# Twenty modulation tiles of a hybrid SSD and MoE block summed by matmuls on TensorE in place of multiply-adds on VectorE

## Chip, cores and metric

The kernel runs on one core of a Trainium2 chip. The metric is device time of one execution in microseconds (us), lower is better; the figure for a kernel is the median of its runs.

## What is computed

Two transformer-like blocks run one after the other over 256 tokens of width 1024, in fp32. Each block starts from a modulation vector that its condition `c` gives; the vector is cut into six pieces of 1024.

```python
# first block
mod = silu(c) @ w_ada + b_ada                      # w_ada: 1024 x 6144
sh1, sc1, g1, sh2, sc2, g2 = split(mod, 6)
h   = layer_norm(x) * (1 + sc1) + sh1
mix = hybrid_mixer(h, ...)                         # SSD branch + short convolution branch
x   = layer_norm(ALPHA * x + g1 * mix) * ln1_g + ln1_b
h   = layer_norm(x) * (1 + sc2) + sh2
x   = layer_norm(ALPHA * x + g2 * moe_ffn(h)) * ln2_g + ln2_b
# second block: mod = silu(c_2) @ w_ada_2 + b_ada_2, six pieces again; attention, convolved feed-forward
```

The mixer projects `h` with `w_in`: the SSD's conv inputs (4096 columns, a causal convolution of four taps and a silu), a short convolution branch (three groups of 1024 columns, then `w_sc_out`), a gate `z` and two merge gates. The change is about the sums `silu(c) @ w_ada`, for twelve pieces in all.

## The kernel before

All weights come through one stream (`Stream`, L35): tiles of 1 MB (128 x 2048 fp32), loaded by DMAs of the SP queue in the order in which they were requested, into five buffers `wraw`. A buffer is given back when its tile is used up, and the next load waits for that. A tile of a projection carries 256 output columns. It is split in two halves, each into a rounded part `whi` on ScalarE (L196) and a rest `wlo` on VectorE (L200), three buffers of each; `lin_fm` (L548) then runs 24 matmuls per half of 128x128 weights against 256 tokens, three for each of eight k (whi by xh, whi by xl, wlo by xh; L556 to L558). A half is split one half ahead of its use.

The stages that matter, with their places in the span:

- start, up to 36 us: the first two modulation pieces (sh1, sc1), with one tile of weights for two rows-of-128 of `w_ada`. `ada_piece` (L395) sums them on TensorE: per tile eight fp32 matmuls of 32 output rows each, four beside each other in four strips of 32 columns of the array, with the activation broadcast to 32 columns in `cst` (L186) as weights;
- conv inputs, 36 to 144 us: sixteen pairs `xbc_pair` (L621), each one `lin_fm` and then, deferred, the taps on VectorE (L633, six per pair);
- convolution, 144 to 239 us: twelve `lin_fm` (pc, ph, pb; L729), and between them steps of the SSD, a generator (`ssd`, L654) that `step` moves on: masks R on GpSimd, `seg`/`ea` matmuls, exponentials E and Cs on ScalarE, products on VectorE (L691, L706), the `yp` matmuls (L713, L717) that read both;
- branch output, 239 to 283 us: four `lin_fm` (pyb, L765) and the rest of the SSD, whose tail runs on to 288 us beside the first `z` matmuls;
- z, the merge gates, the SSD output projection (pya, L868; to 440 us), and the output matmuls pmix (L912) with `w_o`, which VectorE first multiplies by g1 (L242).

The other ten pieces, forty tiles, are put into the stream between these tiles by the strings `XS, SS, OS, ZS, GS, US` (L270): a 1 at place i puts one tile behind the i-th projection tile of that stage. `ada_tick` (L410) uses it up behind that place's `lin_fm`: a multiply by a per-row scalar into the accumulator `adac` for the first of a piece's eight rows-of-128 (ScalarE, L430), a multiply-add for the others (VectorE, L432), 1024 columns wide for the first seven pieces and in two halves of 512 for the last three. Behind the fourth tile four matmuls with a matrix of ones sum the accumulator over the partitions (L437), VectorE adds the bias (L392) and a DMA of ScalarE's queue writes the row out (L461).

Only SP's order is written out by hand in these stages; the order on the other engines is the framework's schedule from the program's order. TensorE and VectorE then work their queues in order.

Of the kernel before, what the change touches and what calls it, by code (L numbers as in the profile page):

```python
# [18 lines left out]
F32 = mybir.dt.float32  # L19
# [102 lines left out]
def build(ctx, tc, I, out, dbg=None, stop=None):  # L122
# [8 lines left out]
    glob = keep  # L131
# [51 lines left out]
    PE.transpose(pt[:, :16], crow, ident[:16, :16])  # L183
    csil = glob.tile([128, 16], F32, name="csil")
    A.activation(csil, pt[:, :16], AF.Silu)
    cst = glob.tile([128, 8, 32], F32, name="cst")  # L186
    V.tensor_copy(cst, csil[:, :8, None].to_broadcast([128, 8, 32]))


    def splitter(q, hi, lo, v):  # L190
# [70 lines left out]
    def req_ada(b, piece):  # L261
        for k0 in range(0, 8, 2):
# [5 lines left out]
    req_ada(0, 1)  # L268

    XS, SS, OS, ZS, GS, US = [[int(c) for c in a] for a in  # L270
                              "0110110110110110,010101010101,1111,11111111,11111111,10101010".split(",")]
    ada_at = {("x", i): XS[i] for i in range(16)}
    ada_at.update({("s", i): SS[i] for i in range(12)})
    ada_at.update({("o", i): OS[i] for i in range(4)})
# [3 lines left out]
    assert sum(ada_at.values()) == 40  # L278
    ada_tiles = [(b, pc, k0) for b, pc in [(0, n) for n in range(2, 6)] + [(1, n) for n in range(6)] for k0 in range(0, 8, 2)]
    ada_next = [0, 0]  # L280
    ADA_WIDE = 7
    ada_acc = [None, None]

# [106 lines left out]
    def ada_end(b, pc, p):  # L390
        r = work.tile([128, 256], F32, tag="adar", name=f"adar{b}_{pc}", bufs=2)
        V.tensor_add(r, p[:, :256], bada[pc % 2])  # L392
        return r

    def ada_piece(b, pc):  # L395

        ada_bias(b, pc)
        p = paux(f"ada{b}_{pc}")
        for k0 in range(0, 8, 2):
            i = ada_q[b, pc, k0]  # L400
            w = ws.take_raw(i)
            wv = w.rearrange("p (k n) -> p k n", k=2)
            for k in range(2):
                for j in range(4):
                    PE.matmul(p[32 * j:32 * j + 32, :256], cst[:, 8 * b + k0 + k, :], wv[:, k, 256 * j:256 * j + 256],
                              start=(k0 + k == 0), stop=(k0 + k == 7), tile_position=(0, 32 * j))
            ws.done(i)
        return ada_end(b, pc, p)

    def ada_tick(*at):  # L410

        for _ in range(ada_at.get(at, 0)):
            b, pc, k0 = ada_tiles[ada_next[1]]
            n = ada_next[1] // 4
            ada_next[1] += 1
            if k0 == 0:
                ada_bias(b, pc)
                if n < ADA_WIDE:
                    ada_acc[:] = [adac[:, n % 2, 512 * h:512 * h + 512] for h in range(2)]
                else:  # L420
                    ada_acc[:] = [work.tile([128, 512], F32, tag="E", name=f"adae{n}_{h}", bufs=3) for h in range(2)]
            i = ada_q[b, pc, k0]
            wv = ws.take_raw(i).rearrange("p (k n) -> p k n", k=2)
            wide = [(adac[:, n % 2, :], slice(0, D))] if n < ADA_WIDE else \
                [(ada_acc[h], slice(512 * h, 512 * h + 512)) for h in range(2)]
            for k in range(2):
                c = csil[:, 8 * b + k0 + k:8 * b + k0 + k + 1]
                for acc, s_ in wide:
                    if k0 + k == 0:
                        A.activation(acc, wv[:, k, s_], AF.Copy, scale=c)  # L430
                    else:
                        V.scalar_tensor_tensor(acc, wv[:, k, s_], c, acc, op0=OP.mult, op1=OP.add)  # L432
            ws.done(i)
            if k0 == 6:
                p = paux(f"ada{b}_{pc}")
                for j in range(4):
                    PE.matmul(p[32 * j:32 * j + 32, :256], ones_r.bitcast(F32)[:, :32],  # L437
                              ada_acc[j // 2][:, 256 * (j % 2):256 * (j % 2) + 256],
                              start=True, stop=True, tile_position=(0, 32 * j))
                ada_row(ada_end(b, pc, p), b, pc)  # L440
# [1553 lines left out]
```

## Time and profile before

| | |
|---|---|
| median of 3 runs | 1335.69 us (1335.33 to 1337.22) |
| the profiled execution | 1335.36 us |
| its span | 1333.5 us |
| TensorE matmul busy | 1265.9 us, 95% |
| VectorE busy | 813.2 us, 61% |
| ScalarE busy | 562.3 us, 42% |
| mean granted TensorE clock | 0.981 |

The span is that from the first to the last instruction. Busy time of TensorE's matmuls overlaps, since they are pipelined and their ends are modelled, so a busy share near 100% does not say by itself that nothing more fits; the step from one matmul's start to the next does. Each fp32 matmul stands in the trace as two records. L432 is line 432 of the kernel, `adac<-wraw,csil,adac` names what is written and what is read, and "idle before <- releaser" is the time for which an engine sat idle, with what ended that.

### The profile page before, as it was taken

The page shows a single profiled execution, that of the slowest core. Times are in us where ns is not written, and L with a number is a line of the kernel's source. Part 1 is how long each engine was busy: PE and PEld are TensorE (multiplying, and loading weights), DVE is VectorE, ACT ScalarE, POOL GpSimd, SP SyncE. Part 2 cuts the span into 40 slices and gives each one's busy share as a digit, 9 for nine tenths or more (in the row PEclk, how much of TensorE's full clock was granted, in tenths as well). Part 3 has the DMA queues.
Part 4 walks back from the last instruction along what each step waited for, and adds up shares of the span by engine and source line. Part 5 has one row for each costly group of instructions (what it writes and reads, how often), then busy time and mean ns, then how long its engine had stood idle before and what let it go on. Part 6 is the DMA issues. An engine that isn't in the chain of part 4 may idle for free.

```text
span 1333.5 us, 22547 instructions
## 1 busy us (share of the span) xinstructions
PE 1265.9 (95%) x8998; PEld 1026.6 (77%) x8998; DVE 813.2 (61%) x1306; ACT 562.3 (42%) x849; POOL 178.3 (13%) x169
## 2 busy tenths in 40 slices
PE   4999999999999989999999999999979998999997
PEld 2989988789899777657576767476548876999985
DVE  2999998977898852222322222222255677788995
ACT  1666644455654341313131313132245655666643
POOL 1001243421100000211112111112120000000000
PEclk9899999999999969999999999999989999999999
DMA  9977867669789287999999999999995334455450
GB/s 338 323 232 254 263 220 239 226 196 320 250 281 362 78 352 296 406 417 419 419 418 413 400 418 419 378 421 403 418 347 179 126 127 141 144 190 190 161 187 32
DMA packets 148975, 380.18 MB, mean 285 GB/s; under 512 B 7839, under 2 KB 97285, under 8 KB 129028
## 3 DMA queue, kind: packets, MB, share of 16 engines
q1 hardware_dynamic: 145856, 373.20, 75.7%
q0 software_dynamic: 2240, 5.34, 1.2%
q8 instruction: 71, 1.16, 0.4%
q10 hardware_dynamic: 772, 0.19, 0.1%
q14 instruction: 36, 0.29, 0.1%
HBM read 377.59 MB, written 1.10 MB: 284 GB/s over the span
## 4 chain that ended last, share of the span: by engine, by line
PE 61%; DVE 5%; DMA 3%; issue 2%; ACT 1%; POOL 0%; POOLq 0%; DVEq 0%; SPq 0%; ACTq 0%
PE gu L1444 16%; PE dn L1475 8%; PE xgp L1402 5%; PE sc L1497 4%; PE pgt L556 2%; PE pgt L557 2%; PE pgt L558 2%; PE pvl L557 2%; PE pvl L556 2%; PE pvl L558 2%; PE pf L908 1%; PE pf L910 1%; PE pf L906 1%; DVE wlo L200 1%; DMA wraw<-in_w_down_dram 1%
## 5 line engine op out<-in xcount | busy, mean ns | idle before, releaser
L196 ACT ACTIVATE whi<-wraw 128x1024 fp32r<-128x1024 f32 x216 | 228.2, 1059 | 239.6 <-PE pf L910 30.8
L200 DVE TENSOR_TENSOR wlo<-wraw,whi 128x1024 fp32r<-128x1024 f32 x216 | 271.4, 1259 | 64.4 <-ACT whi L196 63.0
L1444 PE MATMUL gu<-mraw,xg 128*32 128x256 f32 (+2 forms) x976 | 135.1, 381 | 0.0
L1485 POOL TENSOR_TENSOR y<-yf,y 128x512 fp32r<-128x512 f32 x60 | 76.9, 1282 | 420.8 <-ACT y L1484 420.7
L1454 DVE SCALAR_TENSOR_TENSOR act<-act,gc,gu 128x256 f32<-128x256 f32 x31 | 14.9, 480 | 192.9 <-ACT act L1453 192.9
L1484 ACT ACTIVATE y<-yf 128x512 fp32r<-128x512 f32 x62 | 39.1, 630 | 160.4 <-DVE yf L1483 160.4
L1444 PEld LDWEIGHTS gu<-mraw,xg 128*32 128x32 f32 (+2 forms) x976 | 86.7, 135 | 22.7 <-issue 5.3
L1444 PE MATMUL gu<-wraw,xg 128*32 128x256 f32 (+2 forms) x704 | 98.7, 381 | 0.0
L1483 DVE TENSOR_TENSOR yf<-dn,g 128x512 f32<-128x512 f32 x62 | 42.9, 692 | 66.2 <-PE dn L1475 66.2
L558 PE MATMUL pl<-hh,wlo 128*128 128x256 f32 x256 | 74.3, 291 | 4.2 <-DVE wlo L200 4.1
L1444 PEld LDWEIGHTS gu<-wraw,xg 128*32 128x32 f32 (+2 forms) x704 | 58.2, 129 | 24.1 <-issue 3.9
L556 PE MATMUL pl<-hh,whi 128*128 128x256 f32 x256 | 73.7, 288 | 0.0
L557 PE MATMUL pl<-hl,whi 128*128 128x256 f32 x256 | 73.5, 288 | 0.0
L432 DVE SCALAR_TENSOR_TENSOR adac<-wraw,csil,adac 128x1024 f32<-128x1024 f32 x49 | 66.4, 1355 | 5.1 <-DMA wraw<-in_w_ada_dram 4.5
L1497 PE MATMUL sc<-y,S 128*128 128x512 f32 x248 | 63.3, 404 | 1.4 <-ACT y L1484 0.8
L1497 PEld LDWEIGHTS sc<-y,S 128*128 128x128 f32 x248 | 45.5, 188 | 17.7 <-issue 4.4
L1453 ACT ACTIVATE act<-gu 128x256 f32<-128x256 f32 x31 | 11.9, 384 | 107.3 <-PE gu L1444 107.3
L1404 ACT ACTIVATE xg<-xgp,mvp 128x512 f32<-128x512 f32 (+1 forms) x64 | 48.8, 765 | 19.4 <-PE xgp L1402 19.2
L1402 PE MATMUL xgp<-D,x2h 128*128 128x512 f32 (+1 forms) x128 | 55.5, 434 | 1.4 <-DVE D L1121 1.4
L1475 PE MATMUL dn<-mraw,aT 128*32 128x512 f32 (+2 forms) x200 | 55.4, 596 | 0.0
L558 PEld LDWEIGHTS pl<-hh,wlo 128*128 128x128 f32 x256 | 49.5, 194 | 6.2 <-DVE wlo L200 5.8
L1402 PE MATMUL xgp<-D,x2l 128*128 128x512 f32 (+1 forms) x128 | 53.8, 421 | 0.1
(575 smaller groups left out, 3522.8 us busy)
## 6 DMA issues: line engine op xcount, KB each, us to landing
wraw<-in_w_in_dram SPq DMA_DIRECT2D x56, 1024.0 KB, 6.2
wraw<-in_w_ada_dram SPq DMA_DIRECT2D x47, 1024.0 KB, 7.6
wraw<-in_w_up_dram SPq DMA_DIRECT2D x44, 1024.0 KB, 5.3
wraw<-in_w_down_dram SPq DMA_DIRECT2D x37, 1024.0 KB, 10.0
mraw<-in_w_up_dram SPq DMA_DIRECT2D x32, 1024.0 KB, 14.5
mraw<-in_w_gate_dram SPq DMA_DIRECT2D x28, 1024.0 KB, 7.1
mraw<-in_w_down_dram SPq DMA_DIRECT2D x23, 1024.0 KB, 17.4
wraw<-in_w_gate_dram SPq DMA_DIRECT2D x21, 1024.0 KB, 15.1
```

What stands on the lines that cost most here:

```text
L196: A.activation(hi, v, AF.Copy)
L200: V.tensor_sub(lo, v, hi.bitcast(F32))
L432: V.scalar_tensor_tensor(acc, wv[:, k, s_], c, acc, op0=OP.mult, op1=OP.add)
L556: PE.matmul(o, wh[:, k, :], xh[:, k0 + k, :], start=(k == 0), stop=False)
L557: PE.matmul(o, wh[:, k, :], xl[:, k0 + k, :], start=False, stop=False)
L558: PE.matmul(o, wl[:, k, :], xh[:, k0 + k, :], start=False, stop=(k == 7))
L1402: PE.matmul(p[:, :c1 - c0], src[:, t, j::8], Dt[:, t, c0:c1], start=(q == 0), stop=(q == 3))
L1404: A.activation(xg[:, j, c0:c1], p[:, :c1 - c0], AF.Identity, scale=mvp[:, 1, j:j + 1], bias=mvp[:, 0, j:j + 1])
L1444: PE.matmul(p[c * k:c * k + c, off:off + 256], xg[:, j, 128 * bb + c * k:128 * bb + c * k + c], wt[j], start=(j == 0), stop=(j == 7), tile ...
L1475: last_dn[0] = PE.matmul(pd[h][c * k:c * k + c, :], aT[:, j, c * k:c * k + c], wt[j][:, 512 * h:512 * h + 512], start=(j == 0), stop=(j == ...
L1485: last_sub[0] = (V if b >= LAST else G).tensor_sub(y[:, 1, hs_], yf[:, h, :], y[:, 0, hs_].bitcast(F32))
L1497: PE.matmul(p, St[:, bb + m, 128 * t:128 * t + 128], y[:, k, 512 * h:512 * h + 512], start=(q == 0), stop=(q == 2 * len(ys) - 1))
```

## The change

Of the forty tiles, the twenty of the first five pieces (g1, sh2, sc2, g2 of the first block, the first piece of the second) are summed as at the start: eight matmuls per tile, 160 in all, into one accumulator in PSUM that stays open over the piece's four tiles. It uses the PSUM bank of the tag "acc". The multiply-adds and the reduction matmuls of these five pieces go. The weights of these matmuls are now the activation's column itself, read 32 times by a broadcast; the tile `cst` and the copy that fills it go, for the first two pieces too. The places shift: twelve tiles beside the conv inputs (ten before), four beside the convolution (six before), four beside the branch output as before, so that the twenty of the first five pieces lie in these three stages. The twenty others stay on VectorE; the last four of them move one place back, behind the second half of each SSD output projection instead of behind the first.

```diff
--- before.py
+++ after.py
@@ -183,8 +183,6 @@
     PE.transpose(pt[:, :16], crow, ident[:16, :16])
     csil = glob.tile([128, 16], F32, name="csil")
     A.activation(csil, pt[:, :16], AF.Silu)
-    cst = glob.tile([128, 8, 32], F32, name="cst")
-    V.tensor_copy(cst, csil[:, :8, None].to_broadcast([128, 8, 32]))
 
 
     def splitter(q, hi, lo, v):
@@ -268,7 +266,7 @@
     req_ada(0, 1)
 
     XS, SS, OS, ZS, GS, US = [[int(c) for c in a] for a in
-                              "0110110110110110,010101010101,1111,11111111,11111111,10101010".split(",")]
+                              "0111101111011110,011011000000,1111,11111111,11111111,01010101".split(",")]
     ada_at = {("x", i): XS[i] for i in range(16)}
     ada_at.update({("s", i): SS[i] for i in range(12)})
     ada_at.update({("o", i): OS[i] for i in range(4)})
@@ -278,6 +276,7 @@
     assert sum(ada_at.values()) == 40
     ada_tiles = [(b, pc, k0) for b, pc in [(0, n) for n in range(2, 6)] + [(1, n) for n in range(6)] for k0 in range(0, 8, 2)]
     ada_next = [0, 0]
+    ADA_PE = 5
     ADA_WIDE = 7
     ada_acc = [None, None]
 
@@ -392,19 +391,23 @@
         V.tensor_add(r, p[:, :256], bada[pc % 2])
         return r
 
+    def ada_rows(p, b, pc, k0):
+
+        i = ada_q[b, pc, k0]
+        wv = ws.take_raw(i).rearrange("p (k n) -> p k n", k=2)
+        for k in range(2):
+            c = csil[:, 8 * b + k0 + k:8 * b + k0 + k + 1].to_broadcast([128, 32])
+            for j in range(4):
+                PE.matmul(p[32 * j:32 * j + 32, :256], c, wv[:, k, 256 * j:256 * j + 256],
+                          start=(k0 + k == 0), stop=(k0 + k == 7), tile_position=(0, 32 * j))
+        ws.done(i)
+
     def ada_piece(b, pc):
 
         ada_bias(b, pc)
         p = paux(f"ada{b}_{pc}")
         for k0 in range(0, 8, 2):
-            i = ada_q[b, pc, k0]
-            w = ws.take_raw(i)
-            wv = w.rearrange("p (k n) -> p k n", k=2)
-            for k in range(2):
-                for j in range(4):
-                    PE.matmul(p[32 * j:32 * j + 32, :256], cst[:, 8 * b + k0 + k, :], wv[:, k, 256 * j:256 * j + 256],
-                              start=(k0 + k == 0), stop=(k0 + k == 7), tile_position=(0, 32 * j))
-            ws.done(i)
+            ada_rows(p, b, pc, k0)
         return ada_end(b, pc, p)
 
     def ada_tick(*at):
@@ -415,6 +418,14 @@
             ada_next[1] += 1
             if k0 == 0:
                 ada_bias(b, pc)
+            if n < ADA_PE:
+                if k0 == 0:
+                    ada_acc[0] = pacc(f"ada{b}_{pc}")
+                ada_rows(ada_acc[0], b, pc, k0)
+                if k0 == 6:
+                    ada_row(ada_end(b, pc, ada_acc[0]), b, pc)
+                continue
+            if k0 == 0:
                 if n < ADA_WIDE:
                     ada_acc[:] = [adac[:, n % 2, 512 * h:512 * h + 512] for h in range(2)]
                 else:
```

## Rows read from the trace of the kernel before

**Rows 1.** The page: busy time by engine; VectorE's busy tenths in 40 equal slices

```profile
PE 1265.9 (95%) x8998; PEld 1026.6 (77%) x8998; DVE 813.2 (61%) x1306; ACT 562.3 (42%) x849; POOL 178.3 (13%) x169
...
DVE  2999998977898852222322222222255677788995
```

**Rows 2.** Busy by stretch: conv inputs; convolution; branch output with the SSD's tail

```profile
core 0: us, PE busy (x) PEld busy (x) DVE busy (x) ACT busy (x) POOL busy (x), PEclk, DMA share, GB/s
35.70:143.70 108.00, 103.78 (x824) 100.53 (x823) 101.23 (x170) 70.46 (x97) 10.96 (x8) 0.96 0.82 271
143.70:239.10 95.40, 90.40 (x760) 85.04 (x760) 90.71 (x108) 47.34 (x68) 33.92 (x22) 1.00 0.72 231
239.10:288.20 49.10, 44.08 (x362) 37.65 (x361) 43.39 (x47) 19.82 (x33) 18.79 (x16) 1.00 0.65 215
```

**Rows 3.** Busy by stretch, same columns: matmuls without a stall; half clock

```profile
57.50:69.00 11.50, 11.50 (x97) 11.40 (x95) 11.50 (x18) 6.83 (x11) 0.00 (x0) 1.00 0.98 319
...
101.70:105.10 3.40, 3.14 (x14) 3.14 (x15) 3.40 (x5) 1.19 (x2) 3.09 (x2) 0.50 0.96 344
```

**Rows 4.** Groups by line, 35.7 to 288.2 us, VectorE: busy, mean ns | idle before

```profile
L200 DVE TENSOR_TENSOR wlo<-wraw,whi 128x1024 fp32r<-128x1024 f32 x67 | 89.5, 1340 | 7.0 <-ACT whi L196 6.9
L432 DVE SCALAR_TENSOR_TENSOR adac<-wraw,csil,adac 128x1024 f32<-128x1024 f32 x41 | 56.1, 1368 | 2.1 <-DMA wraw<-in_w_ada_dram 1.9
```

**Rows 5.** TensorE timeline: start, us; last modulation piece at start, one reduction later

```profile
22.31 1.07 PE L405 MATMUL ada<-wraw,cst 128*32 128x256 f32 x16
...
24.30 1.93 PE L405 MATMUL ada<-wraw,cst 128*32 128x256 f32 x32
...
76.92 0.28 PE L556 MATMUL pl<-hh,whi 128*128 128x256 f32 x1
77.13 0.64 PE L437 MATMUL ada<-adac,ones_r 128*32 128x256 f32 x8
77.70 0.38 PE L557 MATMUL pl<-hl,whi 128*128 128x256 f32 x1
```

**Rows 6.** Who waited for whom, 35 to 143 us: us, times, longest

```profile
PEld pl L558 <- DVE wlo L200: 5.8, 7, 3.1
```

**Rows 7.** The same, 143 to 239 us

```profile
PEld yp L717 <- issue: 4.3, 2, 2.3
PE yp L717 <- DVE Cs L706: 3.9, 2, 2.1
...
PEld ada L437 <- DVE adac L432: 0.5, 1, 0.5
```

**Rows 8.** The same, 239 to 289 us

```profile
PE yp L717 <- DVE Cs L706: 2.3, 2, 1.4
PEld yp L713 <- DVE E L691: 2.3, 3, 1.6
...
PEld btp L698 <- issue: 0.9, 1, 0.9
```

**Rows 9.** VectorE timeline, convolution: start, us, what it ran

```profile
220.00 2.07 DVE L432 SCALAR_TENSOR_TENSOR adac<-wraw,csil,adac 128x1024 f32<-128x1024 f32 x1
221.99 2.06 DVE L200 TENSOR_TENSOR wlo<-wraw,whi 128x1024 fp32r<-128x1024 f32 x1
223.97 0.68 DVE L706 TENSOR_TENSOR Cs<-Cs,BC 128x512 f32<-128x512 f32 x1
```

**Rows 10.** VectorE timeline, output matmuls: start, us [idle before <- releaser]

```profile
413.33 1.42 DVE L432 SCALAR_TENSOR_TENSOR adae<-wraw,csil,adae 128x512 f32<-128x512 f32 x2 [3.33 <-DMA wraw<-in_w_ada_dram]
...
436.86 0.42 DVE L392 TENSOR_TENSOR adar<-ada,bada 128x256 f32<-128x256 f32 x1
...
457.16 0.69 DVE L1028 SCALAR_TENSOR_TENSOR xb<-xb,pmix 128x512 f32<-128x512 f32 x1 [2.72 <-PE pmix L910]
```

**Rows 11.** Who waited for whom, 0 to 36 us

```profile
PEld ada L405 <- DMA wraw<-in_w_ada_dram: 4.3, 4, 1.9
...
PEld ada L405 <- DVE cst L187: 0.9, 1, 0.9
```

## The prediction

> **What bounds the kernel now.** I read the page first. TensorE is busy for 95% of the span, and VectorE's busy tenths stand at 7 to 9 over the first thirteen slices, some 430 us, and mostly at 2 in the MoE [rows 1]. The change lies in that first stretch, so I cut it by stage [rows 2]: conv inputs 108.0 us with VectorE busy for 101.2, convolution 95.4 us with 90.7, branch output and SSD tail 49.1 us with 43.4. VectorE is nearly full in all three. TensorE's busy time is nearly full as well, but it contains the drain of pipelined matmuls, so the step between matmuls decides: 97 matmuls in 11.50 us without a stall [rows 3], 0.119 us each, 5.7 us for the 48 of a weight tile. Sixteen tiles make 91 of the conv inputs' 108 us. So there TensorE is nearly full too, and its holes are what VectorE's lateness leaves. Both engines bound this stretch, one just behind the other: work moved from VectorE to TensorE closes the holes that it pays for and adds its own time.
>
> **The change part by part.** *Off VectorE.* A piece has eight rows-of-128, one on ScalarE and seven on VectorE, so five pieces free 35 multiply-adds. At a mean 1368 ns [rows 4] that is 47.9 us off a queue that is busy for 235.3 of 252.5 us (the sums of rows 2). VectorE drops to about 74% and no longer bounds these stages. This time is not the gain: only TensorE's holes are.
>
> *Onto TensorE.* A reduction, eight records, delays the matmul stream from 76.92 to 77.70, 0.78 us, where an ordinary step takes 0.12: it costs 0.66 us [rows 3, 5]. Thirty-two records of the same shape took 1.93 us and sixteen 1.07 [rows 5], so sixteen more cost 0.86 and eight 0.43. A tile of eight matmuls, sixteen records, thus costs 0.66 + 0.43 = 1.09 us; twenty cost 21.8 us. The bounds are 0.86 (no cost at the borders) and 1.32 (two visits of eight records). The five reductions that go save 5 x 0.66 = 3.3 us. Net +18.5 us, on the path, since the tiles stand in TensorE's own queue.
>
> The border shows in the rows: the first record of the reduction starts 0.21 us after the matmul before it and the next matmul 0.57 us after that [rows 5], where 0.12 and 0.43 would be the plain steps. The Trainium skill, TensorEngine Tiling (Array Packing), section Key Properties, says that changing the tiling mode, not just the tile, drains TensorE; that speaks against this change, which makes forty such switches. The trace agrees, with 0.23 us for a pair of them, and the price of a tile from the rows has them in it already; a drain of the full 0.28 us of a matmul at each border would make it 0.86 + 0.56 = 1.42 us and the sum 6.6 us worse.
>
> *Holes beside the conv inputs.* TensorE waited 5.8 us, in seven places, for `wlo` [rows 6], and one wait was followed by 3.40 us at half clock [rows 3], which costs half of that, 1.7 us. Sixteen splits and taps without the multiply-adds fit easily under the matmuls, so I take both back: -7.5 us (bounds -5.8 and -7.5).
>
> *Holes beside the SSD.* In the convolution the `yp` matmuls waited for Cs: 4.3 us on the weight loads and 3.9 on the matmuls, the same places seen twice, so 4.3; and 0.5 for a reduction's input [rows 7]. In the branch output 2.3 for Cs and 2.3 for E [rows 8]. Together 9.4 us. How much is the multiply-adds' doing? One place read in full: a multiply-add from 220.00 (2.07 us), a split behind it (2.06) and only then Cs at 223.97 [rows 9]. Without the first, Cs comes 2 us earlier and the 2 us stall there is gone. E and Cs also have an exponential and a mask before them which stay. I take 90%, -8.5 us (bounds half of it, -4.7, and all, -9.4).
>
> *Holes of other kinds.* The new matmuls need a landed tile and nothing of VectorE, so one may fall into a wait that remains, such as the 0.9 us before `btp` [rows 8]: -1.0 us (bounds 0 and -2).
>
> *The shift in the last four tiles.* The last tile's four half multiply-adds (two in 1.42 us, so 2.8) and the bias add (0.42) now come after the last projection, at about 440 us instead of before 437, and the output matmuls' splits queue behind them on VectorE. VectorE later idles 2.72 us for the first output matmuls [rows 10], which covers most of 3.3 us but not in time for every split: +1.0 us (bounds 0 and +3.3).
>
> *At nothing.* The `cst` copy: TensorE waited 0.9 us for it, and 4.3 us for the same pieces' tiles to land afterwards [rows 11]; the landing hides the earlier start, and without that cover it would give 0.9. ScalarE loses five multiplies; it is busy for 42% of the span [rows 1], and none of the waits of TensorE read here ends on it. The bias DMAs on GpSimd's queue and the row DMAs on ScalarE's stay as many. SP's queue: same 1 MB loads, two of them earlier; a buffer is now given back when TensorE has read it instead of VectorE. New waits: the matmuls wait for the tile's landing, with the whole projection stream queued behind them on TensorE (a rival, below), and a piece's first matmul for the bias add of the piece before, since there is one accumulator; at least one place without a tile lies between two pieces, 5.7 us of matmuls that hide a bias add of 0.42 us [rows 10], and without them it would cost about 1 us a piece.
>
> The sum: +18.5 - 7.5 - 8.5 - 1.0 + 1.0 = +2.5 us on the profiled execution's own 1335.36 us: 1337.9. That execution lies 0.33 us under the median, which I leave out of account. I predict 1338.0 us, 2.3 us or 0.17% slower. What follows shifts as a whole: the later stages start from the end of this chain.
>
> **The rivals.** *Full recovery, faster.* If all 9.4 us beside the SSD come back, borders cost nothing (twenty tiles at 0.86: -4.6 us), 2 us of other holes are filled and the shift is free, the sum is +18.5 - 4.6 - 7.5 - 9.4 - 2 = -5.0: 1330.4. For it: every hole named waits on VectorE, and VectorE gets a quarter of its time back. Against it: the border is seen in the trace. With part of it, the case spans 1330 to 1333.
>
> *TensorE waits for landings, slower.* On VectorE a late tile had other work before and behind it; VectorE once sat 3.33 us for one [rows 10]. On TensorE the whole stream stands still. Five places beside the conv inputs now carry nine loads of 1.05 MB, 9.44 MB in 5 x 5.7 + 4 x 1.09 = 32.9 us, 287 GB/s, where the DMAs gave 319 GB/s at 0.98 busy [rows 3]. It decides from the point where the stream falls below 287. Three such waits of 3.33 us add 10 us: 1348; one, 1341.
>
> *VectorE stays full, slower.* The freed time might be taken by the twenty tiles that remain, since the scheduler already ran 41 - 35 = 6 of their multiply-adds before 288 us [rows 4]. The holes beside the SSD would then come back half: 1342. Against it: the five buffers bound how early a tile can be there.
>
> **How the numbers follow.** A run of this kernel tells 0.2%, 2.7 us, from no change. The forecast's own case (0.50) spreads over 1334 to 1342: 0.28 within 0.2% (up to 1338.4), 0.20 slower, 0.02 faster. Full recovery 0.27, faster. Waits for landings 0.15 and VectorE still full 0.08, slower. Faster 0.29, same 0.28, slower 0.43. The bounds of the unknown costs add to -5.0 and to +18.5 + 4.6 - 5.8 - 4.7 + 3.3 = +15.9 us; the range takes all of the low end, and leaves out the high end, where every bound would be met at once: 1330 to 1345.
>
> **What would show it.** Right: the multiply-adds down by 35; 320 records of the new matmuls, 16 to a tile, at about 1.1 us per tile; VectorE near 185 of 250 us in the three stages; no wait for `wlo` beside the conv inputs, and that stage 3 to 6 us longer while the other two together are 4 or 5 us shorter; no half clock near 102 us. Wrong: waits of TensorE for `w_ada` tiles, waits for Cs and E as long as before, tiles at 1.4 us, or an end of the output matmuls that moves by more than the stages before it.

## The result and the profile after

The changed kernel takes 1348.43 us (median of 5 runs, 1345.62 to 1350.10) against 1337.22 us for the kernel before on the same chip (5 runs, 1335.33 to 1339.42): a ratio of 1.0071, 95% interval [1.0049, 1.0093]. It is slower, by 0.7%. The profiled executions, 1348.74 and 1335.36 us, lie 13.4 us apart, and 1.9 us of that is that the execution of before lies under its median. The forecast was 1338.0 us with a range of 1330 to 1345; the time lies 3.4 us above the range.

The page, TensorE and VectorE, answering [rows 1]:

```profile
PE 1287.7 (96%) x9278; PEld 1038.5 (77%) x9278; DVE 775.1 (58%) x1270; ACT 554.9 (41%) x842; POOL 170.2 (13%) x169
...
DVE  2787877777887971222322222222245677788995
```

VectorE is emptier, 775 us for 813, and TensorE has 280 more records: 320 for the twenty tiles, less 40 for five reductions. The busy times by stage follow; the first three rows answer [rows 2], and the two others are the merge gates and the SSD output projection. After the columns of engines come the granted clock, the DMA share and GB/s.

```profile
core 0: us, PE busy (x) PEld busy (x) DVE busy (x) ACT busy (x) POOL busy (x), PEclk, DMA share, GB/s
35.90:146.98 111.08, 111.08 (x986) 102.09 (x986) 86.44 (x157) 63.96 (x90) 6.75 (x7) 0.98 0.87 290
146.98:243.68 96.70, 95.62 (x821) 88.25 (x820) 73.11 (x91) 45.66 (x66) 31.39 (x24) 1.00 0.55 176
243.68:293.62 49.94, 47.77 (x417) 39.19 (x415) 34.91 (x40) 20.33 (x34) 17.02 (x16) 1.00 0.63 214
344.42:402.16 57.74, 56.01 (x419) 51.88 (x418) 49.84 (x72) 32.13 (x41) 3.89 (x6) 0.94 0.79 258
402.16:453.54 51.38, 48.59 (x393) 47.84 (x392) 43.08 (x54) 21.96 (x27) 1.83 (x3) 0.97 0.81 285
```

A stage runs here from its first projection matmul to that of the next stage; the branch output runs to the first `z` matmul behind the SSD's tail. Against before, conv inputs are longer by 3.1 us (111.08 for 108.03), the convolution by 1.3, the branch output by 0.9: 5.2 us in the three stages that the change is about, with VectorE at 194.5 of 257.7 us, 75%. The merge gates are longer by 4.1 us (57.74 for 53.68), the SSD output projection by 3.6 (51.38 for 47.82), and pmix shorter by 1.2. So more than half of the loss lies in stages in which no matmul was added.

Not only the tiles changed places between the first two stages. In before, the first thirteen matmul records of the SSD run beside the conv inputs, from 121.5 us on; in after all of them stand in the convolution. One of their groups in before and after (behind the durations stand the first and last start; the convolution begins at 143.8 and 147.0 us):

```profile
L659 PE MATMUL cbp<-BC x32: 272/275/377, 121.5 to 272.0; 128*128 128x128 f32 x32
```

```profile
L670 PE MATMUL cbp<-BC x32: 272/275/377, 152.7 to 278.7; 128*128 128x128 f32 x32
```

By the steps from each of the thirteen to the next record this is 2.2 us of TensorE's time that left the conv inputs for the convolution, in every kernel below that has tiles on TensorE.

**Where the changed stages stand.** One visit to a modulation tile in TensorE's timeline, where [rows 5] gave the price, and beside it the reduction of before again, with one more step:

```profile
85.32 0.28 PE L569 MATMUL pl<-hh,wlo 128*128 128x256 f32 x1
85.53 1.07 PE L401 MATMUL ada<-wraw,csil 128*32 128x256 f32 x16
86.53 0.39 PE L567 MATMUL pl<-hh,whi 128*128 128x256 f32 x1
86.75 0.28 PE L568 MATMUL pl<-hl,whi 128*128 128x256 f32 x1
```

```profile
77.92 0.28 PE L558 MATMUL pl<-hh,wlo 128*128 128x256 f32 x1
```

Sixteen records take 1.07 us, as at the start. From the matmul before the visit to the second one behind it are 1.43 us, where two steps of 0.12 would be, so a visit costs 1.19 us, as do ten of the twelve visits beside the conv inputs to 0.01 us; beside the SSD's small matmuls it is 1.0 to 1.3, and one tile there is cut in two visits by the wait for `vv` below. The last 0.10 is the step behind the first projection matmul, 0.22 us. The reduction had that too (77.70 to 77.92), so it cost 0.76.

What TensorE still waits for, answering [rows 7 and 8]; conv inputs have no such row for `wlo`, where [rows 6] had 5.8 us. First the convolution, then the branch output:

```profile
PE yp L728 <- DVE Cs L717: 1.0, 1, 1.0
...
PEld pyb L568 <- DVE vv L499: 1.7, 1, 1.7
...
PEld yp L724 <- DVE E L702: 0.7, 1, 0.7
...
PE yp L728 <- DVE Cs L717: 0.6, 1, 0.6
```

The 1.0 us on Cs stands again as 1.2 on the weight load. With `vv`, E and Cs about 4.2 us remain of what was 9.4. VectorE's groups in these stages show the multiply-adds gone, 4 for 41 [rows 4]:

```profile
L198 DVE TENSOR_TENSOR wlo<-wraw,whi 128x1024 fp32r<-128x1024 f32 x67 | 86.1, 1285 | 44.5 <-ACT whi L194 42.2 <-PE ea L714 1.7 <-PE ada L401 0.3
L443 DVE SCALAR_TENSOR_TENSOR adac<-wraw,csil,adac 128x1024 f32<-128x1024 f32 x4 | 5.1, 1278 | 1.5 <-ACT adac L441 1.5
```

**Where the later stages lose.** In the merge gates TensorE waits for the root of the group norm, `rsh`: 1.0 us before, 1.7 after. First the row of before, then after's, then after's busy times and granted clock (0.50) right behind it, and at 429 us:

```profile
PE prs L808 <- ACT rsh L488: 1.0, 1, 1.0
```

```profile
PE prs L819 <- ACT rsh L499: 1.7, 1, 1.7
```

```profile
core 0: us, PE busy (x) PEld busy (x) DVE busy (x) ACT busy (x) POOL busy (x), PEclk, DMA share, GB/s
364.40:371.20 6.80, 6.80 (x28) 5.90 (x28) 4.25 (x8) 2.80 (x4) 0.00 (x0) 0.50 0.55 169
429.30:432.70 3.40, 3.40 (x18) 3.40 (x17) 3.37 (x5) 0.00 (x0) 0.00 (x0) 0.51 0.53 131
```

A granted clock of 0.50 is the lower of the engine's two levels, 1.2 of 2.4 GHz. From 364.4 it costs half of its 6.8 us, so 3.4, and the wait 0.7 more than before: 4.1 us, all of the stage's loss. The root is a reciprocal and a few products on VectorE; the last one, `gs<-gs,gt`, gives `rsh`. In VectorE's timeline (start, us, [idle before <- releaser]), first before, then after, with ScalarE's row that the last wait goes back to:

```profile
349.62 1.74 DVE L825 RECIPROCAL gs<-gs 8x256 f32<-8x256 f32 x1 [0.93 <-ACT gs L824]
...
354.14 0.41 DVE L829 TENSOR_TENSOR gs<-gs,gt 8x256 f32<-8x256 f32 x1
```

```profile
352.11 0.17 DVE L871 TENSOR_SCALAR mvp<-mvp 128x8 f32<-128x8 f32 x1 [1.09 <-DMA mvp<-mod_scr]
352.19 0.41 DVE L834 TENSOR_SCALAR gvar<-pss 8x256 f32<-8x256 f32 x1
...
353.65 2.72 DVE L443 SCALAR_TENSOR_TENSOR adae<-wraw,csil,adae 128x512 f32<-128x512 f32 x4
356.30 1.73 DVE L836 RECIPROCAL gs<-gs 8x256 f32<-8x256 f32 x1
...
362.11 0.75 DVE L443 SCALAR_TENSOR_TENSOR adae<-wraw,csil,adae 128x512 f32<-128x512 f32 x1 [0.88 <-ACT adae L441]
362.78 0.41 DVE L840 TENSOR_TENSOR gs<-gs,gt 8x256 f32<-8x256 f32 x1
```

```profile
361.35 0.73 ACT L441 ACTIVATE adae<-wraw,csil 128x512 f32<-128x512 f32 x1 [1.49 <-DMA wraw<-in_w_ada_dram]
```

Counted from the stage's first matmul (338.83 and 344.42 us), the reciprocal starts at 10.8 us in before and at 11.9 in after: the variance `gvar` stands behind a 1.09 us wait for the row `mvp`, and the reciprocal behind four multiply-adds. From the reciprocal's start to the end of the last product it is 4.9 us in before and 6.9 in after. There a split more is queued, and a multiply-add for which VectorE sits idle for 0.88 us: its tile landed late, and ScalarE, which forms the tile's first row, had waited 1.49 us for it.

In the output projection it is one load. VectorE's timeline again, and who waited:

```profile
426.55 0.75 DVE L443 SCALAR_TENSOR_TENSOR adae<-wraw,csil,adae 128x512 f32<-128x512 f32 x1 [6.72 <-DMA wraw<-in_w_ada_dram]
427.22 1.22 DVE L198 TENSOR_TENSOR wlo<-wraw,whi 128x1024 fp32r<-128x1024 f32 x1
```

```profile
DVE adae L443 <- DMA wraw<-in_w_ada_dram: 6.7, 1, 6.7
...
PE pya L569 <- DVE wlo L198: 2.8, 1, 2.8
```

[Rows 10] had VectorE idle 3.33 us for such a tile; now it is 6.72, and the split queued behind the multiply-add, whose rounded half ScalarE had ready at 422.1 us, comes so late that TensorE stands 2.8 us, followed by the half clock at 429.3.

### The profile page after: what moved, and what is told of

The parts are those of the page before. It is cut to its first block, busy times and chain, and to the rows that moved or that the text cites. A ratio compares the mean times of both kernels' runs of the same rounds, so it can differ in the third digit from the quotient of the medians.

```text
span 1346.7 us, 23095 instructions
## 1 busy us (share of the span) xinstructions
PE 1287.7 (96%) x9278; PEld 1038.5 (77%) x9278; DVE 775.1 (58%) x1270; ACT 554.9 (41%) x842; POOL 170.2 (13%) x169
## 4 chain that ended last, share of the span: by engine, by line
PE 86%; DMA 7%; DVE 4%; ACT 1%; issue 1%; POOL 0%; ACTq 0%; SPq 0%; DVEq 0%; POOLq 0%
PE gu L1455 16%; PE dn L1486 8%; PE xgp L1413 5%; PE sc L1508 4%; DMA wraw<-in_w_ada_dram 3%; PE pl L567 2%; PE pl L569 2%; PE pl L568 2%; PE ada L401 2%; PE pgt L567 2%; PE pgt L568 2%; PE pgt L569 2%; PE pvl L567 2%; PE pvl L568 2%; PE pvl L569 2%; PE pf L919 1%
## 5 line engine op out<-in xcount | busy, mean ns | idle before, releaser
L198 DVE TENSOR_TENSOR wlo<-wraw,whi 128x1024 fp32r<-128x1024 f32 x216 | 267.8, 1241 | 103.1 <-ACT whi L194 99.4
L1464 ACT ACTIVATE act<-gu 128x256 f32<-128x256 f32 x31 | 11.9, 383 | 107.3 <-PE gu L1455 107.3
L1486 PE MATMUL dn<-wraw,aT 128*32 128x512 f32 (+2 forms) x208 | 51.9, 596 | 1.0 <-DMA wraw<-in_w_down_dram 1.0
L567 PEld LDWEIGHTS pl<-hh,whi 128*128 128x128 f32 x256 | 49.0, 191 | 4.2 <-issue 3.7
```

Source lines behind the costliest of these rows:

```text
L198: V.tensor_sub(lo, v, hi.bitcast(F32))
L567: PE.matmul(o, wh[:, k, :], xh[:, k0 + k, :], start=(k == 0), stop=False)
L1486: last_dn[0] = PE.matmul(pd[h][c * k:c * k + c, :], aT[:, j, c * k:c * k + c], wt[j][:, 512 * h:512 * h + 512], start=(j == 0), stop=(j == ...
```

## The experiments

The lengths of the stages in all kernels of this section, in us, each from its first projection matmul to the next stage's, read from TensorE's timeline (the branch output to the first `z` matmul behind the SSD's tail); "early" is the sum of conv inputs, convolution and branch output. The ratio is that of the medians to the kernel before on the same chip. The last columns are TensorE's wait for `rsh` in the merge gates, and the stretch at half clock in these.

```
kernel    conv in  convol  branch  early   gates  SSD out  pmix   ratio [95%]              rsh  half
before     108.03   95.39   49.06  252.5   53.68   47.82  26.18   1                        1.0  0
b_again    108.55   97.11   49.03  254.7   55.58   47.63  26.66   1.0009 [0.9989, 1.0029]  1.4  3.4
after      111.08   96.70   49.94  257.7   57.74   51.38  25.03   1.0071 [1.0049, 1.0093]  1.7  6.8
e1         111.56   96.70   49.94  258.2   57.90   48.35  26.17   1.0049 [1.0032, 1.0066]  1.9  6.8
e2         108.55   98.85   49.05  256.5   53.94   50.88  25.41   1.0015 [0.9995, 1.0035]  1.2  0
e3         108.95   99.04   49.09  257.1   56.24   48.21  26.25   1.0035 [1.0017, 1.0053]  1.7  3.4
e4         113.02   96.62   48.12  257.8   53.99   51.31  25.41   1.0027 [1.0011, 1.0043]  1.3  0
e5         111.25   96.70   49.94  257.9   56.48   49.67  26.16   1.0055 [1.0034, 1.0076]  1.5  6.8
e6         106.12   94.71   49.67  250.5   55.68   48.20  26.16   0.9957 [0.9940, 0.9974]  1.1  3.4
e7         109.59   95.92   50.89  256.4   51.73   50.15  26.17   1.0014 [0.9997, 1.0031]  0.2  0
e8         102.51   97.40   47.85  247.8   53.69   48.02  26.17   0.9932 [0.9906, 0.9959]  1.0  0
e9         111.56   96.70   49.93  258.2   58.13   48.14  26.18   1.0037 [1.0019, 1.0055]  2.1  6.8
e10        111.54   96.70   49.94  258.2   52.12   55.80  25.76   1.0070 [1.0046, 1.0094]  0    0
e11        103.84  100.38   49.04  253.3   57.59   47.99  26.49   1.0003 [0.9986, 1.0020]  1.9  6.8
```

The conv inputs hold one more thing that differs between executions. By the granted clock, each has half clock from some point between 30 and 36 us on, and it reaches into the conv inputs by 4.55 us in before, 2.47 in e8, 5.43 in e11 and 3.3 to 5.4 in the others; it costs half of that.

### Which part of the change costs what: e1, e2, e3, e4, and before once more

e1 is the changed kernel with the last four tiles back at their places:

```diff
-  "0111101111011110,011011000000,1111,11111111,11111111,01010101"
+  "0111101111011110,011011000000,1111,11111111,11111111,10101010"
```

> The changed kernel with one string put back: the last four modulation tiles again behind the first half of each SSD output projection. Theory A, the loss of the late stages is the shift of these four tiles: the SSD output projection falls from 51.4 to about 48 us, the 6.7 us wait of VectorE for a modulation tile goes to 3.3 or less, and the kernel is about 3.5 us faster than the changed one: 1.004 to 1.005 of before. Theory B, the late stages only follow from TensorE's extra time and the order it brings: 1.007 of before as with the whole change.

The output projection goes from 51.38 to 48.35 us and pmix from 25.03 to 26.17, so the shift cost 1.9 us net. VectorE's longest wait for a tile there is 3.9 us, and of TensorE's wait for `wlo` 0.9 us are left, in two places:

```profile
DVE adae L443 <- DMA wraw<-in_w_ada_dram: 4.4, 2, 3.9
...
PE pya L569 <- DVE wlo L198: 0.9, 2, 0.7
```

The rest of the loss stays: the three stages at 258.2, the gates at 57.90.

e2 is the kernel before with that shift alone:

```diff
-  "0110110110110110,010101010101,1111,11111111,11111111,10101010"
+  "0110110110110110,010101010101,1111,11111111,11111111,01010101"
```

> The kernel before with that one string of the change: only the last four tiles move one place back, all on VectorE. Theory A: the SSD output projection grows from 47.8 us by 3 to 5 us, 1.002 to 1.004 of before. Theory B: 1.000, the stage within 0.5 us of 47.8.

The projection takes 50.88 us, 3.1 more than before, and pmix gives 0.8 back: 2.3 us, and the medians say 1.0015. The wait is the same, without any of the new matmuls:

```profile
DVE adae L432 <- DMA wraw<-in_w_ada_dram: 6.4, 1, 6.4
...
PE pya L558 <- DVE wlo L200: 2.3, 1, 2.3
```

Both ways round, the shift costs about 2 us.

e3 is the changed kernel with all places of before, so that only the engine of the twenty tiles changes; e4 has the new places and every tile on VectorE:

```diff
# e3
-  "0111101111011110,011011000000,1111,11111111,11111111,01010101"
+  "0110110110110110,010101010101,1111,11111111,11111111,10101010"
# e4
-    ADA_PE = 5
+    ADA_PE = 0
```

> The changed kernel with all the places of before (10 tiles beside the conv inputs, 6 beside the convolution, 4 beside the branch output, the last four where they were): the change of engine alone. From the price of 1.2 us per tile and the holes as they closed with the whole change, the three early stages come to 252.5 + 5.2 = 257.7 us. Theory A: late stages as before, 1.004. Theory B: late stages longer too, by some 7 us, 1.007 to 1.009.

> The changed kernel with all forty tiles on VectorE: the change of places alone. Twelve tiles beside the conv inputs, where VectorE is full: that stage grows by two tiles of multiply-adds, 2 x 2.5 = 5 us, to 113, and the convolution falls by up to as much. Theory A: the late stages lose 3 to 5 us as with the whole change, 1.002 to 1.005. Theory B: about 1.000.

The engine alone costs 1.0035, and its three stages take 257.1 us, as long as with the new places (257.7): the early places hardly matter once the tiles are on TensorE. On VectorE they matter: with twelve tiles beside the conv inputs in place of ten, that stage takes 113.0 us (e4), 5.0 more than before. The two parts, 1.0035 and 1.0027, add to 1.0062, near the 1.0071 of the whole.

The kernel before was run once more as a kernel of its own (b_again), for the spread between profiled executions:

> The kernel before once more, on the chip of these runs, for a trace beside them. The three early stages at 252.5 us give or take 2 us of half clock, merge gates at 53.7, SSD output projection at 47.8.

The medians agree, and the stages show what one profile can't tell. This execution has half clock at 102.6, 184.5 and 362.0 us, 3.4 us each, where the first had it at 101.7 alone; its early stages take 254.7 us, its merge gates 55.58 after a wait of 1.4 us for `rsh`. e2, which changes nothing before the output projection, has half clock at 103.5, 185.4 and 229.8 us and early stages of 256.5. So the same code takes 252.5 to 256.5 us there. At 1.7 us for each stretch of 3.4, one and two more stretches make 1.7 and 3.4 us of the differences of 2.2 and 4.0; nearly all the rest is the half clock of the start, which reaches 0.8 us further, 0.4 us. The profiled execution that the forecast started from is the quickest of the three. With the twenty tiles on TensorE and the new places the early stages are steady, 257.7 to 258.2 us in five executions (after, e1, e5, e9, e10), none with half clock in the middle of them: the change costs 5.2 us against the first execution, and 1.2 to 3.5 against the two others. Of after's loss in the gates, half is what the unchanged kernel can show too.

### What a tile costs on TensorE: e6, e7

e6 is e1 with only one of each tile's two rows-of-128 summed by the new matmuls:

```diff
-        for k in range(2):
+        for k in range(nk):
...
-                ada_rows(ada_acc[0], b, pc, k0)
+                ada_rows(ada_acc[0], b, pc, k0, 1)
```

> As e1_last_back, but of each of the twenty tiles only the first of its two rows-of-128 is summed (half of the new matmuls are left out; the tiles are still loaded and waited for). If TensorE's own time is on the path one for one, twenty times 0.43 us, 8.6 us, go from the early stages, 249 instead of 258 us, and the kernel is at 0.998 to 0.999 of before. If something else (landings, the SSD's chain, VectorE) set their length, they stay above 255 us and the kernel near 1.005.

The three stages take 250.5 us in place of 258.2: 7.7 us less for 160 records fewer, which at eight records per 0.43 us would be 8.6. Of the 7.7, 0.5 is the half clock of the start, which reaches 1.1 us less far here. More than eight tenths of the new matmuls' own time is on the path. The start of the same execution is 1.9 us longer than in e1 and the gates 2.2 shorter; the medians differ by 0.9%.

e7 is e1 with the tiles in pairs, two behind one projection tile, so that there are ten visits less to the other form of matmul:

```diff
-  "0111101111011110,011011000000,1111,11111111,11111111,01010101"
+  "0020200202002020,020020000000,0202,11111111,11111111,10101010"
```

> As e1_last_back, but the twenty tiles come in ten pairs at every second or third place, so that TensorE changes to the 32-column strips ten times and not twenty. The trace gives 1.19 us for a visit of one tile, of which 0.86 is matmuls: ten borders less, 3.3 us. Theory border price: early stages 3 us shorter, 1.002 to 1.003 of before. Rival: two modulation tiles in a row in a ring of five buffers make the projections' loads late, TensorE waits for `whi` or for landings, and the gain is lost: 1.005 or more.

The early stages gain 1.8 us, 0.18 per visit saved, where the timeline's border is 0.33 (1.19 less the 0.86 of the matmuls). Part of the gain is the half clock of the start again, 0.66 us. Without it the conv inputs give back 1.3 us (1.97 less 0.66), which is what their visits, read one by one, are shorter by (14.06 less 12.76); but the branch output is 1.0 us longer. Each border costs something, but not all of it comes back. The total, 1.0014 against 1.0049, gains more than that, and the table has the place: hardly a wait for `rsh` in the gates (0.2 us), which take 51.73 us. That is a coincidence of the order there and not the price of a border.

### The merge gates: e5, e9, e10

e5 is e1 with the gates' tiles moved away from the root: none at the first two places, two each at the third and fourth.

```diff
-  "0111101111011110,011011000000,1111,11111111,11111111,10101010"
+  "0111101111011110,011011000000,1111,11111111,00221111,10101010"
```

> As e1_last_back, but the two modulation tiles beside the first two merge-gate projections are moved two places on, so that no multiply-add stands on VectorE between the steps of the group norm's reciprocal root. Theory C, the multiply-adds that the schedule put into that chain hold it back: the wait of TensorE for the root falls from 1.9 to under 1 us, no half clock follows, and the merge gates take at most 54 us in place of 57.9; the kernel is 3 to 4 us faster than e1_last_back, 1.002 of before. Theory D, the merge gates are longer for another reason (the modulation row's DMA, a later landing): 57 us as in e1_last_back and 1.005.

The chain was not cleared by that: VectorE had four multiply-adds of earlier tiles ahead of the reciprocal there too and two behind it, the wait for `rsh` is 1.5 us and the half clock 6.8. So this run tells nothing apart.

e9 is e1 with the add on `mvp`, which waits for a DMA ahead of `gvar`, held back until the root is done; e10 holds the multiply-adds behind the second gate's tile back as well:

```diff
+    with tc.issue_after(ws.root.ins):            # e9, e10
         V.tensor_scalar(mvp[:, 1, :], mvp[:, 1, :], 1.0, None, op0=OP.add)
...
+    with ExitStack() as st:                      # e10
+        if at == ("g", 1):
+            st.enter_context(tc.issue_after(ws.root.ins))
         V.scalar_tensor_tensor(acc, wv[:, k, s_], c, acc, op0=OP.mult, op1=OP.add)
```

> As e1_last_back, but the one instruction that adds 1 to a modulation row loaded by a DMA stands behind the group norm's root on VectorE, and not in front of it, where it waited 1.0 us for its DMA. Theory C, order on VectorE in front of the root sets the merge gates' loss: the root comes 1.0 us earlier, TensorE's wait for it falls from 1.9 to about 0.9 us, and the half clock behind it goes or gets shorter: merge gates 53.5 to 55 us in place of 57.9, 1.002 to 1.004. Theory D, other things: 57 us and more, 1.005.

> As e9_root_first, and the four multiply-adds of the tile beside the second merge-gate projection, which stood in one row of 2.7 us in front of the root's reciprocal, are held until the root is done. Theory C: the reciprocal starts when its input is there, 1.2 us earlier still, TensorE hardly waits (under 0.5 us), no half clock: merge gates 52 to 53 us, 1.000 to 1.002. Theory D: no change from e1_last_back, 1.005.

Without the wait for `mvp` (e9) the reciprocal starts 10.8 us into the stage again, as in before, but the wait for `rsh` stays, 2.1 us: that DMA alone isn't the cause. With the multiply-adds held back as well (e10), nothing waits for `rsh`, the half clock is gone and the gates take 52.12 us, 6.0 less than e9, though TensorE now waits there for `wlo`, 2.5 us in two places with the full clock behind them (first row of the fence on waits below). VectorE's timeline tells which multiply-adds matter, first e9, then e10:

```profile
355.64 1.73 DVE L836 RECIPROCAL gs<-gs 8x256 f32<-8x256 f32 x1
...
362.86 0.75 DVE L443 SCALAR_TENSOR_TENSOR adae<-wraw,csil,adae 128x512 f32<-128x512 f32 x1 [2.28 <-ACT adae L441]
```

```profile
356.79 1.74 DVE L839 RECIPROCAL gs<-gs 8x256 f32<-8x256 f32 x1 [2.48 <-ACT gs L838]
...
361.76 0.41 DVE L843 TENSOR_TENSOR gs<-gs,gt 8x256 f32<-8x256 f32 x1
```

The stage starts at 344.78 us in e9 and at 346.00 in e10, so the reciprocal comes 10.8 us behind that in e10 too: the four multiply-adds ahead of it, gone there, had cost it next to nothing in e9 (0.2 us: ScalarE's square root, which the reciprocal takes, ended at 355.46 there). What got shorter is the stretch from the reciprocal's start to the end of the last product, 5.4 us in e10 for 8.3 in e9. In e9 VectorE stands there for 2.28 us before a multiply-add of the next tile, whose first row ScalarE had not formed; in e10 that tile comes behind the root. So it is a tile that landed late, queued on VectorE ahead of the last product, that keeps the root back. No run moves that one tile alone; e10 does it by holding the tile before it. The unchanged kernel has the same wait in b_again, 0.37 us, and not in the first execution. But the total is no better, 1.0070, since the loss moves on. For the output projection follow VectorE's timeline, TensorE's waits (the first row is that of the gates), and its granted clock (the 0.50 of the row's last columns):

```profile
434.88 0.75 DVE L446 SCALAR_TENSOR_TENSOR adae<-wraw,csil,adae 128x512 f32<-128x512 f32 x1 [2.33 <-DMA wraw<-in_w_ada_dram]
```

```profile
PE pg L572 <- DVE wlo L198: 2.5, 2, 1.7
...
PE pya L572 <- DVE wlo L198: 1.7, 1, 1.7
```

```profile
438.30:441.70 3.40, 3.40 (x18) 3.40 (x18) 3.40 (x5) 1.01 (x3) 0.00 (x0) 0.50 0.96 316
```

The held tiles give their buffers back later, a tile lands later, and the output projection takes 55.80 us, 7.7 more than in e9. The work is deferred, not removed.

### How many tiles are worth it: e8, e11

e8 keeps every place of before and puts two pieces on TensorE, eight tiles: four beside the conv inputs (behind the pairs 7, 8, 10 and 11, counted from 0) and the convolution's last four. e11 does so with the first of these pieces alone.

```diff
-    ADA_PE = 5
+    ADA_PE = (1, 3)        # e11: (1,)
...
-            if n < ADA_PE:
+            if n in ADA_PE:
```

> The places of before, and only two of the five pieces (the second, beside the conv inputs, and the fourth, beside the convolution: eight tiles) summed on TensorE, three on VectorE. Price 8 x 1.19 less two reductions of 0.76, 8.0 us. If the holes close in proportion (8 of 20 tiles of the 14.8 us got back), 5.9 us come back: early stages 254.6 us, 1.001 to 1.002. If the first tiles taken off a full VectorE close most of the holes, 10 us or more come back: early stages 250 us, 0.998 to 0.999 of before and the best version.

> As e8_two_pieces, with only the second piece (four tiles beside the conv inputs) summed on TensorE: price 4 x 1.19 less one reduction, 4.0 us. With two pieces the early stages came to 247.8 us, 4.7 less than before, so 8.0 us of price closed 12.7 of the 17 us of holes. If the first tiles close most, the 7.4 us beside the conv inputs close here and the SSD's mostly stay: early stages 249 to 250 us, 0.997 to 0.998 of before. If a place in the convolution did it, 252 us and 1.000.

e8 takes 1330.84 us, 0.9932 of before, better than both kernels. Its granted clock from conv inputs to pmix, and the wait for Cs in the convolution and the branch output:

```profile
39.00:469.00 430.00, 417.98 (x3375) 384.68 (x3374) 371.65 (x521) 230.31 (x311) 75.94 (x74) 1.00 0.76 252
```

```profile
PE yp L728 <- DVE Cs L717: 2.1, 3, 1.0
```

e11 takes 1340.38 us, the same as before. The conv inputs gain almost as much, but the convolution is 5.0 us longer than in before. 2.2 of that are the SSD's matmuls from beside the conv inputs, and two stretches of half clock make 3.4; it waits more for Cs than before did (5.2 us for 3.9), and VectorE waits for tiles:

```profile
PE yp L728 <- DVE Cs L717: 5.2, 2, 3.3
DVE adac L443 <- DMA wraw<-in_w_ada_dram: 3.9, 2, 2.4
```

```profile
182.80:186.20 3.40, 3.40 (x25) 3.07 (x22) 2.02 (x6) 0.91 (x2) 0.00 (x0) 0.50 0.69 270
227.20:230.60 3.40, 3.40 (x19) 3.40 (x18) 1.60 (x4) 1.06 (x1) 0.00 (x0) 0.50 0.45 125
```

What was closed of the conv inputs' holes is worked out from these terms: the cost of the visits there, each read in the timeline (five visits for four tiles in e8 and e11, since two tiles were cut into three visits), less that of the reductions saved; less the change of the stage; plus half of what the half clock of the start reaches further into it than in before; less the SSD's matmuls that went to the convolution.

```
        tiles there   visits less reductions   stage   start's clock   SSD moved   holes closed
e11          4              4.72               -4.19      +0.44          2.17          7.18
e8           4              4.72               -5.52      -1.04          2.17          7.03
e3          10             10.15               +0.92      +0.11          2.17          7.17
after       12             12.54               +3.05      -0.16          2.17          7.16
```

Four tiles close all that can be closed there, 7.0 to 7.2 us, and every further one only costs its price. Beside the SSD, at 1.19 us for a tile and 0.76 for a reduction, 4 x 1.19 - 0.76 - 0.8 = 3.2 us, and 5.4 with the 2.2 moved there, are closed by e8's four tiles, and 8 x 1.19 - 2.28 - 2.2 = 5.0, and 7.2 with the 2.2, by after's eight, against the first execution. e11, which moves none there, is 5.0 us longer in the two stages than that execution and 1.5 longer than that of e2, which also has two stretches of half clock there; its three early stages are 3.2 us shorter than those of e2. That e8 is 10.6 us faster than before between medians goes, by the table and b_again, to 6.9 us in the early stages, 1.9 in the gates and the rest behind; which of these differences belong to e8, and which to the half clock of the execution compared, isn't settled.

## Why the prediction was right or wrong

**Right in kind.** The tiles cost TensorE's time nearly in full (e6), the visits are near 1.1 us, the wait for `wlo` beside the conv inputs and the half clock at 102 us are gone, VectorE is at 75%, and the conv inputs are longer by the 3 to 6 us that were named, at 3.1, though only since 2.2 us of the SSD's matmuls left them. Of the rivals, full recovery fell: of the 9.4 us of waits beside the SSD about 4.2 are left. VectorE staying full fell too. TensorE's waits for landings did not happen; no TensorE wait in the three stages is for a tile of `w_ada`.

**The tile's price: 1.09 forecast, 1.19 measured.** The step behind the visit was counted to the first projection matmul and not to the second, which is late by another 0.10 us; the reduction was short by the same. Net +20.0 us (23.8 less 3.8) in place of +18.5. The Trainium skill, TensorEngine Tiling (Array Packing), section Key Properties, says that a change of the tiling mode drains TensorE; the timeline agrees, with 0.33 us for the two switches of a visit, between the 0.23 of the forecast and the 0.56 of two full drains.

**The holes: -17.0 forecast, -14.8 measured.** By stage it looks like 9.7 us closed beside the conv inputs for the 7.5 forecast, and 5.0 beside the SSD for 9.5 (8.5 and the 1.0 of other holes). But 2.2 us of it only changed sides, with the SSD's first matmuls, which the list of stages ahead of the prediction has in the convolution. Without them it is 7.5 and 7.2; against the two other executions of the unchanged code the second is 8.9 and 10.7, and these have 1.7 and 3.4 us of half clock beside the SSD. So the term of the conv inputs came out, and that of the SSD was 2.3 us too large. One place was read in full [rows 9], and its answer, that the multiply-add ahead was all of the wait, was given to 90% of the others. Of the 9.4 us of waits about 5.2 went, so the bound of half, 4.7, was the better guess for the waits themselves; of the 4.2 left, 1.7 are for `vv`, on which TensorE waited 0.3 us before. Together the early stages came out at +5.2, where the terms for them give +1.5.

**The shift: +1.0 forecast, about 2 measured (e1 1.9, e2 2.3).** Inside its bounds, but by another mechanism than was named. It was priced as work behind the last projection, ahead of pmix's splits; pmix got shorter. What was late was a load: a tile asked for half a place later is not landed when VectorE comes to it, and a wait of 6.7 us blocks the splits queued behind it. The row that shows this wait, 3.33 us [rows 10], was read, and used for a rival on TensorE only. On VectorE such a wait was taken as free, although the splits there feed TensorE.

**Later stages: nothing forecast, +4.1 us in the merge gates.** "What follows shifts as a whole" was wrong. The twenty remaining tiles stand in another order relative to the chains of the later stages, and the gates' root, which had come 1.0 us late already, came 1.7 late, behind the wait for `mvp` and behind a multiply-add whose tile had not landed (e9, e10). That it was followed by half clock gave most of the price. This is the largest of the misses, and of the same kind as the shift's: a late tile on VectorE's queue with work for TensorE behind it. By b_again, about 2 us of the 4.1 can fall to an execution of the unchanged kernel, so the change's own share lies between 2 and 4 us.

The sum by the profiled executions: +20.0 - 14.8 + 2.4 (the output projection with pmix) + 4.1 + 1.5 of small differences elsewhere = 13.2 us, the difference of the two spans. Of the 10.7 us above the forecast's +2.5, 4.1 are thus the later stages put at nothing, 2.2 the holes, 1.5 the price, 1.4 the shift and 1.5 the rest.

**The question that wasn't asked** was how many tiles. Both engines were read as near their limit, rightly, and the price and the holes were then each summed over all twenty. Closed holes do not grow with the tiles, the price does: the sum says that twenty come out near zero, and the same rows would have said that the first four beside the conv inputs, at 4.0 us, find 7.5 us of holes. It would still not have given the whole: e11 has just these four and gains 4.2 us there, but has 5.0 more beside the SSD, by moved work and half clock, and 3.9 more in the gates.

## What to carry to other kernels

When two engines are both nearly full, move work by small steps and set the price of the next piece against the holes that are still open; here eight tiles of twenty made the kernel 0.7% faster, and all twenty made it 0.35% slower at the same places and 0.7% at the new ones. Price a move between queues to the second instruction behind it, and follow every in-order queue that is touched to the loads that it waits for: one late tile on VectorE stopped TensorE by way of the splits behind it. A change in an early stage doesn't leave the later ones as they were; look in the trace for chains there that come late already.

## What the runs showed of the hardware

A short wait of TensorE can cost more by the clock than by itself. In the merge gates seven waits of 1.4 to 2.1 us for `rsh` were each followed by 3.4 or 6.8 us at half clock, of three of 1.1 to 1.3 us only one was, and those of 0.2 to 1.0 us were not (three kernels; e10 has no such wait). The length of the wait isn't all of it: in the convolution of before two waits, the longer 2.1 us [rows 7], had the full clock behind them [rows 2]. And it differs between executions of one kernel: the same wait, as long, was followed by 3.4 us of half clock at 184.5 us in b_again (first row), and b_again has half clock at 362 us (second row), the first execution none there:

```profile
184.25 0.50 PE L717 MATMUL yp<-Cs,st 128*64 128x128 f32 x4 [2.10 <-DVE Cs L706]
...
362.00:365.40 3.40, 3.40 (x18) 3.40 (x17) 3.40 (x7) 1.88 (x4) 0.00 (x0) 0.50 0.90 299
```
